# A decoder layer on one core: more of a threshold search and a square on ScalarE, down weights prepared earlier and kept in DRAM

## The chip, the cores and the metric

One core of a Trainium2 chip. The metric is the device time of one execution in microseconds (us), the median of several runs. PE is TensorE, PEld its weight load, DVE is VectorE, ACT is ScalarE, POOL is GpSimd, SP is SyncE, which issues the DMAs. L12 is line 12 of the kernel.

## The reference, cut to what matters

One layer over 2048 tokens of width 1024 in float32. A query keeps 256 keys, chosen by an indexer's scores; attention runs over those keys; its output is normalised per head. Then comes a SwiGLU with 2816 hidden columns.

```python
score = jnp.where(causal[None], score, NEG_INF)
_, sel = lax.top_k(score, k_sel)                # k_sel = 256
...                                             # attention over the selected keys
attn = group_rms_norm(attn, attn_norm_g, N_HEADS_ATTN)   # x * rsqrt(mean(x*x) + eps) per head
x = layer_norm(DEEPNORM_ALPHA * x + g1[:, None, :] * mix, ln1_g[l], ln1_b[l])
ff = (silu(h @ w_gate) * (h @ w_up)) @ w_down   # h = modulate(x, sh2, sc2)
x = layer_norm(DEEPNORM_ALPHA * x + g2[:, None, :] * ff, ln2_g[l], ln2_b[l])
```

## The kernel before, in words

Tokens are 16 blocks of 128 (P = 128, CH = 512). The program is written as nested generators. A planner, which works with its own costs, turns it into one fixed order of instructions for each engine; every engine then runs its list in order and waits at semaphores. So an instruction that waits holds up all that stands behind it on that engine. The same holds for SP, on whose list nearly all DMAs stand (`dma` is `nc.sync.dma_start`). A tile that takes over memory from another one waits for that tile's last reader.

**Search (`topk`, L458 to 569).** The 256th largest score of every query is found by a threshold search: in each of 8 iterations the columns of a block above the threshold are counted. A block b has n = 128(b + 1) columns. ScalarE counts the last n2 of them with Sign and an accumulator (L512), VectorE the first n1 = n - n2 with a comparison and an accumulator (L514). n2 is one number for a group of blocks; DVE_SHARE = 0.42 sets it. The groups (2 to 5), (6 to 8), (9, 10) are searched early. LATE, (11, 12, 13) and (14, 15), are searched as background work of the attention loop: scores come back from DRAM as tile scb, and `attention` calls `next(background)` once a step.

**Attention (L821 to 1049).** It has 136 steps of one query block and 128 keys: three matmuls for each half of the heads into l, exp on ScalarE into p (L894), its half-precision copy ph (L895), the rest pr on POOL (L897), 24 small matmuls into o (L907 to 909). `maxima` (L863 and 865: TensorE, then a reduction on VectorE) runs ahead for the next blocks. `finish` (L911 to 924) copies o to ov, squares it into asq (L916, VectorE), sums, and scales.

**Feed-forward.** Products are Strassen-like: a 2 x 2 block product in 7 products, HM = (1, 2, 6, 5, 7, 3, 4), whose operands are sums of blocks; each operand is split in a high and a low half-precision part (`split_w`: ACT copy L215, DVE L216), and each product runs as three matmuls. Gate and up: 11 pairs p of hidden tiles, for each two groups of rows, grp 0 and 1, which I call units; a unit is 7 x 2 x 12 = 168 matmuls (L1207). `hidden1` makes products 1, 2, 6, 5, `hidden2` 7, 3, 4. In grp 1 the weights of the next pair are prepared (`prep_w`). `put_g` writes the combined activations to DRAM (go, L1237 to 1242). PSUM has 8 banks, all used in turn.

Down: 8 passes q of 7 products, each 11 pairs times 3 matmuls, so 231 (L1503). The left operands, gi, come back from DRAM into 4 buffers. Pass 0 goes by pieces of pairs (0 to 3, 4 to 7, 8 to 10), all 7 products in each. The 77 right operands stay in SBUF for all passes: 24 tiles wdr where the activations of group 0 lay, 8 wdw in the weight buffers, 2 wdt, 43 wdo in the pool fo, which opens when the pools of gate and up close. `prep_wd` makes them (L1388 to 1407): per pair 4 raw loads, 4 sums on POOL (L1105 to 1112), 7 splits. 24 tiles are asked for after the last unit of group 0, the rest inside pass 0, as needed. Raw buffers, sums, temporaries and output buffers are rings with a few slots each; from the start of gate and up the raw ring has 8 and the output ring 6.

Of the kernel before, what the change touches and what calls it, by code (L numbers as in the profile page):

```python
# [12 lines left out]
F16 = mybir.dt.float16  # L13
# [8 lines left out]
P = 128  # L22
# [120 lines left out]
def body(ctx: ExitStack, tc: tile.TileContext, A, out, force=False):  # L143
# [13 lines left out]
    xn_d = [dram(f"xn_d{b}", [P, D], F32) for b in range(NB)]  # L157
    h2_d = [dram(f"h2_d{b}", [P, KT * P], F32) for b in range(NB)]
    t_d = {m: dram(f"t_d{m}", [P, 2, 4, CH], F16) for m in HM[3:]}
    g_d2 = [{m: dram(f"gg_d{g}_{m}", [P, 4, NP, 2, P], F16) for m in HM} for g in range(2)]  # L160


# [295 lines left out]
    def topk(blocks, scs):  # L458
# [34 lines left out]
        V.scalar_tensor_tensor(hi[:, 0], sd, 8.0, mu, op0=ALU.mult, op1=ALU.add)  # L493
        zero, below = sm("zero")[:, 0], sm("below")[:, 0]

        n2 = int(sum(b + 1 for b in blocks) / nb * P * (1 - DVE_SHARE)) // 64 * 64
        big_at, tgt = TOPK - n2 / 2.0, TGT - n2 / 2.0
        V.tensor_scalar(lo[:, 1], cst(C_N), -n2 / 2.0, None, op0=ALU.add)
        V.memset(hi[:, 1], -n2 / 2.0)
# [6 lines left out]
        for it in range(NITER):  # L506
            for i, b in enumerate(blocks):
                n = (b + 1) * P
                n1 = n - n2
                j1 = tk.tile([P, 1024], BF16, tag="j1", name="j1", bufs=1)  # L510
                j2 = tk.tile([P, 1216], BF16, tag="j2", name="j2", bufs=1)
                S_.activation(j2[:, 0:n2], scs[i][:, n1:n], AF.Sign, bias=t[:, i:i + 1],  # L512
                              scale=-1.0, accum_out=ca2[:, i:i + 1])
                V.tensor_scalar(j1[:, 0:n1], scs[i][:, 0:n1], t[:, i:i + 1], None,  # L514
                                op0=ALU.is_ge, op1=ALU.add, accum_out=cd[:, i:i + 1])
                yield
            V.scalar_tensor_tensor(cnt, ca2, -0.5, cd, op0=ALU.mult, op1=ALU.add)
            V.scalar_tensor_tensor(which, tcur[:, 1:2].broadcast_to([P, 2, nb]), big_at, upper,
                                   op0=ALU.is_ge, op1=ALU.not_equal)
            V.copy_predicated(ends, which.bitcast(I32).unsqueeze(2).broadcast_to([P, 2, 2, nb]),  # L520
                              tcur.unsqueeze(1).broadcast_to([P, 2, 2, nb]))
            if it == NITER - 1:
                break
            V.tensor_tensor(dd, hi, lo, op=ALU.subtract)
            d = dd[:, 0]
            if it == 0:
                V.scalar_tensor_tensor(a, cnt, -tgt, sd, op0=ALU.add, op1=ALU.mult)
                V.tensor_tensor(a, a, cst(C_SL), op=ALU.mult)
                V.tensor_tensor(a, a, t, op=ALU.add)
                V.scalar_tensor_tensor(f, d, 0.02, lo[:, 0], op0=ALU.mult, op1=ALU.add)  # L530
                V.tensor_tensor(a, a, f, op=ALU.max)
                V.scalar_tensor_tensor(f, d, -0.02, hi[:, 0], op0=ALU.mult, op1=ALU.add)
                V.tensor_tensor(t, a, f, op=ALU.min)
            else:
                V.reciprocal(a, dd[:, 1])
                V.scalar_tensor_tensor(f, lo[:, 1], -tgt, a, op0=ALU.add, op1=ALU.mult)
                V.tensor_scalar(f, f, CLIP - 1.0, -CLIP, op0=ALU.max, op1=ALU.min)
                V.tensor_tensor(f, f, d, op=ALU.mult)
                V.tensor_tensor(t, lo[:, 0], f, op=ALU.subtract)
            if it == PROBE:  # L540
                V.tensor_scalar(a, lo[:, 0], 0.0, None, op0=ALU.is_lt)
                V.scalar_tensor_tensor(f, hi[:, 0], 0.0, a, op0=ALU.is_gt, op1=ALU.mult)
                V.copy_predicated(t, f.bitcast(I32), zero)
            if it == PROBE + 1:
                V.tensor_scalar(f, hi[:, 0], 0.0, None, op0=ALU.is_equal)
                V.copy_predicated(t, f.bitcast(I32), below)
            yield
# [273 lines left out]
    def attention(pool=None, background=None, at_block=None, at_end=None):  # L821
# [89 lines left out]
        def finish(b, po):  # L911
            ov = aq[0].tile([P, 2, 4, 65], F32, tag="ov", name=f"ov{b}", bufs=two)
            S_.activation(ov, po[:, :, 0:260].rearrange("p g (h d) -> p g h d", d=65), AF.Copy)
            o3 = ov.rearrange("p g h d -> p (g h) d")
            sq = aq[0].tile([P, H, DH], F32, tag="asq", name=f"asq{b}", bufs=1)
            V.tensor_tensor(sq, o3[:, :, 0:64], o3[:, :, 0:64], op=ALU.mult)  # L916
            ms = ap.tile([P, 2, H], F32, tag="ms", name=f"ms{b}", bufs=2)
            V.tensor_reduce(ms[:, 0], sq, axis=AX.X, op=ALU.add)
            V.tensor_tensor(ms[:, 1], o3[:, :, 64], o3[:, :, 64], op=ALU.mult)
            V.scalar_tensor_tensor(ms[:, 0], ms[:, 1], EPS * DH, ms[:, 0], op0=ALU.mult, op1=ALU.add)  # L920
            root(ap, ms[:, 0], ms[:, 0], 1.0 / DH, None)
            on = ap.tile([P, H, DH], F32, tag="on", name=f"on{b}", bufs=three)
            V.tensor_tensor(on, o3[:, :, 0:64], ms[:, 0].unsqueeze(2).broadcast_to([P, H, DH]), op=ALU.mult)
            return on
# [451 lines left out]
    def wd_slots(R):  # L1376
        for n in range(24):
            yield R.tile([P, 2, CH], F16, name=f"wdr{n}")
        for n in range(8):
            yield wring(f"wdw{n}")  # L1380
        for n in range(2):
            yield outs(f"wdt{n}").rearrange("p a x t -> p (a x t)").rearrange("p (x n) -> p x n", x=2)
        n = 0
        while True:
            yield fo[0].tile([P, 2, CH], F16, name=f"wdo{n}")
            n += 1

    def prep_wd():  # L1388

        R = ff.enter_context(tc.tile_pool(name="fw", bufs=1, side="right", reuse_waits="tile"))  # L1390
        gpool[0] = R
        slots = wd_slots(R)
        for p in range(NP):
            b = []
            for r in range(2):
                for hh in range(2):
                    x = raws(f"wd{p}_{r}{hh}")
                    dma(x, A["wd"][2 * p + r][:, hh * CH:(hh + 1) * CH])
                    b.append(x)
            y = sums(f"yd{p}")  # L1400
            for m in RIGHT:
                x = right(G, b, y, m)
                w = next(slots)
                split_w(w[:, 0], w[:, 1], x)
                wd_tiles[m, p] = w
                yield p

    rows = {}
    fo = [None]
    gpool = [None]  # L1410
    pwd = prep_wd()
    second = prep_h(1)
    for p in range(NP):
        nxt = {}
        pw = prep_w(p + 1, nxt) if p + 1 < NP else iter(())
        for grp in range(2):
            if p == 0 and grp == 0:
                u, v, g11 = heads["u"], heads["v"], heads["g"]
                gate = temps("gate")
                gated(gate, g11, 0)  # L1420
                gated(g11, heads["c"][1], 1, gate)
            else:
                u, v = [temps(f"u{grp}{p}_{x}") for x in range(2)], {}
                g11 = prods(f"g11_{grp}{p}")
                for i, _ in enumerate(hidden1(fbank, Ws, HT[grp], u, v, g11, lambda k, x: temps(f"{k}h{grp}{p}_{x}"))):
                    if grp == 1 and i % 2:
                        if i == 1:
                            next(pw, None)
                        next(pw, None)
            for i, _ in enumerate(hidden2(fbank, Ws, HT[grp], u, v, g11, p, grp)):  # L1430
                if grp == 1 and i % 2 and p:
                    next(pw, None)
                if p == 0 and grp == 0 and i == 0:
                    for _ in second:
                        pass
            if p == NP - 1 and grp == 0:
                early_h[0].close()
                for _ in range(24):
                    next(pwd)
        if p == 0:  # L1440
            few_s.close()
            fq = hid.enter_context(tc.tile_pool(name="fq", reuse_waits="tile", bufs=1))
            wring.slots[8:12] = [(fq, 4)] * 4
        for _ in pw:
            pass
        Ws = nxt
# [44 lines left out]
        G.tensor_tensor(x, x, rows["l1b"][hh], op=ALU.add)  # L1491
        return x

    PIECES = ((0, 4), (4, 8), (8, 11))

    def down(q, m, ps, p0, p1_):
        g = gpool[0].tile([P, 4, 2, P], F16, tag="gi", name=f"gi{q}_{m}{p0}", bufs=4)[:, 0:p1_ - p0]
        dma(g, g_d2[q // 4][m][:, q % 4, p0:p1_])
        for p in range(p0, p1_):
            while (HM[-1], p) not in wd_tiles or (HM[-2], p) not in wd_tiles:  # L1500
                next(pwd)
            for n, (x, y) in enumerate(((0, 0), (0, 1), (1, 0))):
                T.matmul(ps, g[:, p - p0, x], wd_tiles[m, p][:, y], start=p == 0 and n == 0,  # L1503
                         stop=p == NP - 1 and n == 2)
# [1 line left out]
    for q in range(8):  # L1506
        blocks = (q // 4 * 8 + q % 4, q // 4 * 8 + q % 4 + 4)
        banks = {}
        if q == 0:
            banks = {m: fbank() for m in HM}  # L1510
            for piece in PIECES:
                for m in HM:
                    down(q, m, banks[m], *piece)
# [121 lines left out]
```

## Time and profile before

| | us |
|---|---|
| median of 3 runs (2542.55 to 2549.05) | 2543.98 |
| the profiled execution | 2544.64 |
| its span | 2542.8 |
| PE busy | 2319.4 (91%) |
| DVE busy | 1804.2 (71%) |
| ACT busy | 1185.0 (47%) |
| POOL busy | 1230.5 (48%) |

The span is what the profiler recorded from the first to the last instruction. Busy times overlap; an engine that is busy or idle matters only where the next step waits for it. Times inside the kernel are us from the span's start.

### The profile page before, as it was taken

What the parts mean: (1) busy time and instruction counts of PE and PEld (TensorE: products, weight loads), DVE (VectorE), ACT (ScalarE), POOL (GpSimd) and SP (SyncE); (2) the same over time, 40 slices, a digit from 0 to 9 for tenths busy, and PEclk for the clock granted to TensorE, in tenths of its full rate; (3) what the DMA queues carried; (4) which work ended last, traced back from release to release, by engine and by line L of the source; (5) the groups of instructions that cost most, each with busy time, mean ns of one, the idle gap of its engine ahead of it and who ended that gap; (6) DMA issues with size and microseconds to landing.
All of it is one profiled execution on the core that took longest, in us unless ns stands there. A gap on an engine that the chain in (4) does not pass through costs nothing.

```text
span 2542.8 us, 38397 instructions
## 1 busy us (share of the span) xinstructions
PE 2319.4 (91%) x13538; PEld 1119.3 (44%) x13538; DVE 1804.2 (71%) x3649; ACT 1185.0 (47%) x2263; POOL 1230.5 (48%) x1232
## 2 busy tenths in 40 slices
PE   5799999996879699889969999999999986999998
PEld 3444444443444355555424444444444432444443
DVE  8998999989999876763396666776666697422223
ACT  3687776646767566777543233332333343110000
POOL 3000000003655666898376556655655565855455
PEclk9799999998989899999979999999999998999999
DMA  8421442434131322330242223222222236444443
GB/s 272 127 104 68 149 133 89 150 123 144 58 121 60 126 93 81 117 110 29 106 132 88 75 87 92 84 71 75 71 88 79 85 115 207 150 141 148 128 137 121
DMA packets 213917, 281.72 MB, mean 111 GB/s; under 512 B 15825, under 2 KB 128849, under 8 KB 212945
## 3 DMA queue, kind: packets, MB, share of 16 engines
q1 hardware_dynamic: 213712, 279.17, 34.5%
q8 instruction: 107, 1.75, 0.3%
q14 instruction: 98, 0.79, 0.1%
HBM read 183.20 MB, written 95.91 MB: 110 GB/s over the span
## 4 chain that ended last, share of the span: by engine, by line
PE 35%; POOL 6%; DMA 4%; DVE 3%; issue 2%; ACT 0%; SPq 0%; DVEq 0%; POOLq 0%
PE f L1207 30%; PE f L1503 5%; DMA x<-xn_d 2%; POOL z L1480 1%; DMA gi<-gg_d 1%; POOL x L1491 1%; POOL x L1490 1%; POOL z L1547 1%; POOL z L1548 1%; DMA wd<-in_wd 1%; DVE wdo L216 0%; DVE h L1171 0%; DVE z L1536 0%; POOL wd L1112 0%; POOL yd L1105 0%
## 5 line engine op out<-in xcount | busy, mean ns | idle before, releaser
L897 POOL TENSOR_TENSOR pr<-p,ph 128x256 f16<-128x256 f32 x544 | 379.6, 730 | 140.2 <-ACT ph L895 61.2
L1207 PE MATMUL f<-h,wwg 128*128 128x512 f16 x1800 | 419.9, 383 | 25.0 <-ACT h L1170 18.0
L1207 PE MATMUL f<-h,wwu 128*128 128x512 f16 x1800 | 414.1, 380 | 0.0
L1241 POOL TENSOR_TENSOR go<-g,go 128x512 f16<-128x512 f32 x126 | 169.7, 1356 | 274.1 <-ACT go L1240 236.3
L1503 PEld LDWEIGHTS <-gi 128*128 128x128 f16 x1848 | 180.7, 99 | 276.2 <-DMA gi<-gg_d 47.4
L1207 PEld LDWEIGHTS <-wwg 128*128 128x128 f16 x1848 | 182.1, 99 | 232.3 <-issue 14.9
L1207 PEld LDWEIGHTS <-wwu 128*128 128x128 f16 x1848 | 181.1, 98 | 234.2 <-issue 17.0
L1503 PE MATMUL f<-wdo,gi 128*128 128x512 f16 x1032 | 242.1, 386 | 15.6 <-DMA gi<-gg_d 6.8
L865 DVE CUSTOM_DVE_ANT_0 jk<-m,ua 128x512 bf16<-128x512 f32 (+3 forms) x320 | 193.7, 605 | 56.2 <-PE m L863 41.6
L894 ACT ACTIVATE p<-l 128x512 f32<-128x512 f32 x272 | 158.3, 598 | 90.7 <-PE l L890 69.2
L1240 ACT ACTIVATE go<-g 128x512 f16<-128x512 f32 x132 | 82.5, 627 | 230.6 <-issue 82.8
L447 ACT ACTIVATE r<-xs 128x512 f32<-128x512 f32 (+3 forms) x304 | 153.4, 548 | 57.3 <-PE xs L446 14.0
L895 ACT ACTIVATE ph<-p 128x512 f16<-128x512 f32 x272 | 166.5, 635 | 2.9
L909 PE MATMUL o<-vst,pr 128*128 128x65 f16 x1088 | 140.4, 196 | 14.4 <-POOL pr L897 13.7
L1503 PE MATMUL f<-wdr,gi 128*128 128x512 f16 x576 | 136.5, 386 | 16.2 <-DMA gi<-gg_d 16.1
L737 PE MATMUL b<-hi,wch 128*128 128x512 f16 x384 | 146.7, 382 | 0.0
L737 PE MATMUL b<-lo,wch 128*128 128x512 f16 x384 | 146.3, 381 | 0.0
L737 PE MATMUL b<-hi,wcl 128*128 128x512 f16 x384 | 146.3, 381 | 0.0
L907 PE MATMUL o<-vst,ph 128*128 128x65 f16 x1088 | 142.8, 194 | 1.8 <-ACT ph L895 1.8
L908 PE MATMUL o<-vst,ph 128*128 128x64 f16 x1088 | 141.5, 194 | 0.0
L1470 ACT ACTIVATE frs<-fmv,epsw 128x1 f32<-128x1 f32 x16 | 4.7, 294 | 282.3 <-DVE fmv L1467 282.3
L863 PE MATMUL m<-k1T,qst 128*128 128x512 f16 (+3 forms) x320 | 105.4, 360 | 29.5 <-DVE mp L865 26.0
(384 smaller groups left out, 5194.3 us busy)
## 6 DMA issues: line engine op xcount, KB each, us to landing
gg_d<-go SPq DMA_DIRECT2D x154, 256.0 KB, 2.6
gi<-gg_d SPq DMA_DIRECT2D x112, 256.0 KB, 3.0
wa<-in_w_ada SPq DMA_DIRECT2D x64, 256.0 KB, 2.9
wg<-in_wg SPq DMA_DIRECT2D x49, 256.0 KB, 3.0
wu<-in_wu SPq DMA_DIRECT2D x49, 256.0 KB, 3.0
wd<-in_wd SPq DMA_DIRECT2D x44, 256.0 KB, 3.0
gi<-gg_d SPq DMA_DIRECT2D x56, 192.0 KB, 2.8
wa<-in_w_ada SPq DMA_DIRECT2D x16, 512.0 KB, 8.6
```

The lines of the kernel that those rows point to most:

```text
L447: S_.activation(r[:, i:i + e], ps[:, 0:e], AF.Relu)
L737: T.matmul(ps, w[:, k, j * P:(j + 1) * P], x[:, k], start=n == 0, stop=n == 3 * KT - 1)
L865: V.tensor_tensor_reduce(jk[:, 0:w], ps[:, 0:w], u[:, j * 512:j * 512 + w], scale=1.0, scalar=-3e38, op0=ALU.add, op1=ALU.max, accum_out=m ...
L894: S_.activation(p32, pl_, AF.Exp, scale=DH ** -0.5)
L895: S_.activation(ph, p32, AF.Copy)
L897: G.tensor_tensor(pr[:, i:i + CH // 2], p32[:, i:i + CH // 2], ph[:, i:i + CH // 2], op=ALU.subtract)
L907: T.matmul(o, lhs, vst[:, kt, 64:129], start=kt == 0 and hh == 0, stop=False)
L908: T.matmul(o[:, 0:64], lhs, vst[:, kt, 0:64], start=False, stop=False)
L909: T.matmul(o, pr[:, hh * P:(hh + 1) * P], vst[:, kt, 64:129], start=False, stop=kt == b and hh == 3)
L1207: T.matmul(ps, w[:, x, k * P:(k + 1) * P], h[:, y, :, k], start=n == 0, stop=n == 11)
L1241: (V if (p, grp) in LASTG else G).tensor_tensor(o[:, :, 1], x4, o[:, :, 0], op=ALU.subtract)
L1503: T.matmul(ps, g[:, p - p0, x], wd_tiles[m, p][:, y], start=p == 0 and n == 0, stop=p == NP - 1 and n == 2)
```

## The change

Four edits. (a) In the searches of LATE, n2 becomes b0 * P, with b0 the first block of the group: 1408 columns for blocks 11 to 13 and 1792 for 14 and 15. (b) The square in `finish` moves from VectorE to ScalarE. (c) `prep_wd(p)` becomes a generator for one pair; it is stepped beside the products of group 0 of pair p + 1 (for the last pair beside group 1), at every second of their yields, and stores each tile to a DRAM tile wd_d. (d) `load_wd` loads the tiles in the order in which pass 0 uses them: 24 after the last unit of group 0, the others ahead of pass 0, the first 28 of these in fo. In pass 0 the gi loads are issued by ScalarE. The scratch tiles of the counts change their size (j1, j2).

```diff
+    wd_d = {(m, p): dram(f"wd_d{m}_{p}", [P, 2, CH], F16) for m in HM for p in range(NP)}
...
-        n2 = int(sum(b + 1 for b in blocks) / nb * P * (1 - DVE_SHARE)) // 64 * 64
+        if blocks in LATE:
+            n2 = b0 * P
+        else:
+            n2 = int(sum(b + 1 for b in blocks) / nb * P * (1 - DVE_SHARE)) // 64 * 64
...
-                j1 = tk.tile([P, 1024], BF16, tag="j1", name="j1", bufs=1)
-                j2 = tk.tile([P, 1216], BF16, tag="j2", name="j2", bufs=1)
+                j1 = tk.tile([P, 640], BF16, tag="j1", name="j1", bufs=1)
+                j2 = tk.tile([P, 1792], BF16, tag="j2", name="j2", bufs=1)
...
-            V.tensor_tensor(sq, o3[:, :, 0:64], o3[:, :, 0:64], op=ALU.mult)
+            S_.activation(sq, o3[:, :, 0:64], AF.Square)
...
     def wd_slots(R):
         for n in range(24):
             yield R.tile([P, 2, CH], F16, name=f"wdr{n}")
+        for n in range(28):
+            yield fo[0].tile([P, 2, CH], F16, name=f"wdo{n}")
         for n in range(8):
             yield wring(f"wdw{n}")
-        for n in range(2):
-            yield outs(f"wdt{n}").rearrange(...)
-        n = 0
+        n = 28
...
-    def prep_wd():
+    def prep_wd(p):
...
+        yield                                   # after the 4 raw loads
+        y = sums(f"yd{p}")
+        for m in RIGHT:
+            x = right(G, b, y, m)
+            w = outs(f"wdp{p}_{m}").rearrange(...)
+            split_w(w[:, 0], w[:, 1], x)
+            dma(wd_d[m, p], w)
+            yield
+
+    def load_wd():
+        gpool[0] = ff.enter_context(tc.tile_pool(name="fw", bufs=1, side="right", reuse_waits="tile"))
+        slots = wd_slots(gpool[0])
+        for piece in PIECES:
+            for m in HM:
+                for p in range(*piece):
+                    wd_tiles[m, p] = next(slots)
+                    dma(wd_tiles[m, p], wd_d[m, p])
+                    yield
...
+            pd = iter(())
+            if grp == 0 and p:
+                pd = prep_wd(p - 1)
+            elif grp and p == NP - 1:
+                pd = prep_wd(p)
...                                             # in the loops over hidden1 and hidden2:
+                    if i % 2 == 0:
+                        next(pd, None)
...
+            for _ in pd:
+                pass
...
-        dma(g, g_d2[q // 4][m][:, q % 4, p0:p1_])
+        (S_.dma_start if q == 0 else dma)(g, g_d2[q // 4][m][:, q % 4, p0:p1_])
...
-            while (HM[-1], p) not in wd_tiles or (HM[-2], p) not in wd_tiles:
-                next(pwd)
...
             banks = {m: fbank() for m in HM}
+            for _ in pwd:
+                pass
```

## Rows read from the trace of the kernel before

**Rows 1.** Busy time by stage; the first line names the columns.
```profile
core 0: us, PE busy (x) PEld busy (x) DVE busy (x) ACT busy (x) POOL busy (x), PEclk, DMA share, GB/s
...
604.00:860.00 256.00, 204.13 (x1779) 111.87 (x1778) 238.62 (x686) 179.03 (x354) 146.39 (x193) 0.91 0.27 91
860.00:1268.00 408.00, 376.93 (x3662) 214.04 (x3660) 251.45 (x605) 272.67 (x557) 299.09 (x407) 0.99 0.27 93
...
1321.00:1930.30 609.30, 608.77 (x2807) 275.33 (x2807) 416.13 (x499) 198.04 (x340) 353.17 (x253) 0.99 0.28 84
1930.30:1966.50 36.20, 36.20 (x169) 16.46 (x168) 18.76 (x24) 8.98 (x16) 16.05 (x13) 1.00 0.22 66
1966.50:2002.80 36.30, 36.30 (x170) 16.43 (x168) 29.89 (x35) 14.93 (x26) 25.79 (x19) 1.00 0.32 95
...
2039.00:2075.30 36.30, 36.30 (x170) 16.46 (x168) 35.96 (x32) 17.73 (x32) 31.23 (x20) 1.00 0.39 116
2075.30:2168.10 92.80, 62.54 (x227) 23.40 (x225) 70.18 (x84) 35.65 (x62) 48.01 (x32) 0.83 0.52 168
2168.10:2532.60 364.50, 353.41 (x1624) 157.21 (x1622) 104.49 (x171) 33.62 (x55) 198.45 (x154) 1.00 0.47 139
```

**Rows 2.** Waits of PE, 604 to 860: waiter, releaser, us, times, longest.
```profile
PE m L863 <- DVE mp L865: 11.4, 15, 1.9
PE m L875 <- DVE mx L871: 9.6, 4, 6.0
...
PE m L965 <- DVE z L957: 7.6, 4, 4.6
```

**Rows 3.** Groups of DVE by line and shape, 604 to 860: busy us, mean ns, idle before.
```profile
L514 DVE TENSOR_SCALAR_CACHE_REDUCE j<-scb,tc 128x832 bf16<-128x832 f32 x16 | 17.2, 1074 | 0.2
...
L514 DVE TENSOR_SCALAR_CACHE_REDUCE j<-scb,tc 128x960 bf16<-128x960 f32 x8 | 9.7, 1208 | 0.1
L514 DVE TENSOR_SCALAR_CACHE_REDUCE j<-scb,tc 128x704 bf16<-128x704 f32 x8 | 7.4, 930 | 0.0
...
L514 DVE TENSOR_SCALAR_CACHE_REDUCE j<-scb,tc 128x576 bf16<-128x576 f32 x8 | 6.4, 802 | 0.0
L916 DVE TENSOR_TENSOR asq<-ov 128x512 f32<-128x512 f32 x8 | 6.1, 765 | 0.0
```

**Rows 4.** The same view of DVE, 0 to 604.
```profile
L514 DVE TENSOR_SCALAR_CACHE_REDUCE j<-sc,tc 128x192 bf16<-128x192 f32 x8 | 3.3, 410 | 0.2
```

**Rows 5.** The same view of ACT: 604 to 860, and L754 from 0 to 604.
```profile
L512 ACT ACTIVATE j<-scb,tc 128x960 bf16<-128x960 f32 x24 | 26.1, 1090 | 7.2 <-DVE tc L539 4.0 <-DVE tc L546 2.8 <-DVE tc L491 0.3
L512 ACT ACTIVATE j<-scb,tc 128x1088 bf16<-128x1088 f32 x16 | 19.2, 1198 | 7.2 <-DVE tc L543 2.9 <-DVE tc L539 2.5 <-DVE tc L533 1.0
...
L754 ACT ACTIVATE g<-y 128x512 f32<-128x512 f32 x16 | 10.1, 628 | 14.4 <-DVE y L753 14.3
```

**Rows 6.** Groups by line in the last unit, 2039 to 2075.3: DVE, POOL, ACT.
```profile
L216 DVE SCALAR_TENSOR_TENSOR wdr<-wd,wdr 128x512 f16<-128x512 f32 x18 | 24.7, 1398 | 0.1
...
L1110 POOL TENSOR_TENSOR wd<-yd,wd 128x512 f32<-128x512 f32 x4 | 6.8, 1715 | 0.6 <-DVE wdr L216 0.6
...
L215 ACT ACTIVATE wdr<-wd 128x512 f16<-128x512 f32 x20 | 11.7, 622 | 11.6 <-DMA wd<-in_wd 4.8 <-POOL wd L1108 3.9 <-POOL wd L1110 1.9
```

**Rows 7.** SP's queue in order of time: start, duration, DMA issued.
```profile
2076.50 9.23 SPq L1398 DMA_DIRECT2D wd<-in_wd  x4
...
2092.21 0.33 SPq L1498 DMA_DIRECT2D gi<-gg_d  x1
...
2105.92 0.44 SPq L1460 DMA_DIRECT2D l1g<-in_ln_g  x1
```

**Rows 8.** Waits of PE in pass 0, then in passes 1 to 7.
```profile
PE f L1503 <- DMA gi<-gg_d: 21.0, 9, 8.9
...
PE f L1503 <- DMA gi<-gg_d: 10.9, 16, 1.5
```

**Rows 9.** Busy time by stage, columns as in rows 1: a stretch at the kernel's start.
```profile
10.00:40.00 30.00, 18.65 (x88) 10.47 (x89) 29.46 (x62) 9.67 (x17) 8.37 (x8) 0.94 1.07 362
```

More of the change, by code (lines that the diff above doesn't have):

```diff
@@ L1378, in wd_slots @@
             yield R.tile([P, 2, CH], F16, name=f"wdr{n}")
+        for n in range(28):
+            yield fo[0].tile([P, 2, CH], F16, name=f"wdo{n}")
         for n in range(8):
             yield wring(f"wdw{n}")
-        for n in range(2):
-            yield outs(f"wdt{n}").rearrange("p a x t -> p (a x t)").rearrange("p (x n) -> p x n", x=2)
-        n = 0
+        n = 28
         while True:
@@ L1386, in wd_slots @@
             n += 1
-    def prep_wd():
[L1390 to L1406, printed above, removed]
+    def prep_wd(p):
+        b = []
+        for r in range(2):
+            for hh in range(2):
+                x = raws(f"wd{p}_{r}{hh}")
+                dma(x, A["wd"][2 * p + r][:, hh * CH:(hh + 1) * CH])
+                b.append(x)
+        yield
+        y = sums(f"yd{p}")
+        for m in RIGHT:
+            x = right(G, b, y, m)
+            w = outs(f"wdp{p}_{m}").rearrange("p a x t -> p (a x t)").rearrange("p (x n) -> p x n", x=2)
+            split_w(w[:, 0], w[:, 1], x)
[10 more added lines that the diff above has]
+                    yield
     rows = {}
@@ L1410, in body @@
     gpool = [None]
-    pwd = prep_wd()
+    PIECES = ((0, 4), (4, 8), (8, 11))
+    pwd = load_wd()
     second = prep_h(1)
@@ L1432, in body @@
                     next(pw, None)
+                if i % 2 == 0:
+                    next(pd, None)
                 if p == 0 and grp == 0 and i == 0:
@@ L1492, in residual @@
         return x
-    PIECES = ((0, 4), (4, 8), (8, 11))
     def down(q, m, ps, p0, p1_):
         g = gpool[0].tile([P, 4, 2, P], F16, tag="gi", name=f"gi{q}_{m}{p0}", bufs=4)[:, 0:p1_ - p0]
-        dma(g, g_d2[q // 4][m][:, q % 4, p0:p1_])
+        (S_.dma_start if q == 0 else dma)(g, g_d2[q // 4][m][:, q % 4, p0:p1_])
         for p in range(p0, p1_):
-            while (HM[-1], p) not in wd_tiles or (HM[-2], p) not in wd_tiles:
-                next(pwd)
             for n, (x, y) in enumerate(((0, 0), (0, 1), (1, 0))):
```

## Prediction

> **What bounds the kernel now.** I read the stage table first: busy time of each engine, stage by stage, because the share of one engine over the whole span mixes stages with different limits [rows 1]. Four of its rows matter here. In the stage 604 to 860 us, where attention starts while the top-k search of blocks 11 to 15 runs behind it, VectorE is busy 238.62 of 256 us (93%) and ScalarE 179.03: VectorE is the limit. In 860 to 1268 it is TensorE (376.93 of 408). In gate and up TensorE has no gap at all: 608.77 of 609.30, and 36.20 of 36.20 and 36.30 of 36.30 in the units after it. A unit (pair p, row group) is 168 matmuls, so one matmul takes 36.3/168 = 0.216 us. In the down product the first pass (q=0) takes 92.80 us for 231 matmuls, which at 0.216 would be 50; the other seven take 364.50 for 1617, which would be 349. So there are three places where time can be had: the VectorE stage, 43 us of the first pass, 15 us of the other passes.
>
> Second view, the waits. In 604 to 860 the longest waits of TensorE for another engine are for VectorE [rows 2]. In the first pass TensorE waits 21.0 us for activations (gi), not for weights, and in passes 1 to 7 10.9 us [rows 8]. The reader should not stop at the name gi: the queue of SP shows why gi is late. SP is in order, and four raw weight loads occupy it from 2076.50 for 9.23 us, waiting for raw buffers that the preparation of earlier weights still holds; the fifth gi load is only issued at 2092.21, behind them [rows 7]. The first pass is bounded by the preparation of the down weights.
>
> **Part A, the search and the square.** The ScalarE share of the columns rises from 960 to 1408 in blocks 11 to 13, and from 1088 to 1792 in 14 and 15; VectorE keeps 128, 256, 384, 128 and 256 columns. Eight iterations each. VectorE counts these now in 17.2 + 9.7 + 7.4 + 6.4 = 40.7 us [rows 3]; the line through 576 columns (0.802) and 960 (1.208) has 1.057 ns a column, so 128, 256 and 384 columns cost 0.33, 0.46 and 0.60; the row for 192 columns (0.410, the line gives 0.40) bears this out [rows 4]. That makes 8 x 1.39 + 8 x 0.79 = 17.4, so VectorE loses 23.3 us. ScalarE: (1.198 - 1.090)/128 = 0.84 ns a column [rows 5], so 1408 columns take 1.47 and 1792 take 1.79; 24 x 1.47 + 16 x 1.79 = 63.9 in place of 26.1 + 19.2 = 45.3: ScalarE gains 18.6. The square leaves VectorE 8 times in this stage (6.1 us, [rows 3]) and comes to ScalarE at 0.628 each [rows 5], 5.0 us. It follows its input ov on the same engine, so it waits for nobody; behind it stand exponentials, and the reduction on VectorE now waits for it. The other eight squares lie where TensorE is the limit and count nothing.
>
> So VectorE goes to 238.6 - 23.3 - 6.1 = 209, ScalarE to 179.0 + 23.6 = 203, of 256. The gain lies between 0 (the room is filled by ScalarE, whose exponentials now stand behind counts of up to 1.8 us) and the whole 29 us that VectorE loses. Other row: TensorE's three longest waits for VectorE here sum to 28.6 us [rows 2], and 12% of VectorE's work is taken away, which by itself would give back only 3 to 4. I take **12**, about the middle.
>
> The Trainium skill (ScalarE: Activation LUTs, Rules for kernel authors) says that plain arithmetic belongs on VectorE, which it calls up to about three times faster per element in bf16; by that rule this part would gain nothing. The rows differ for these f32 counts: 0.84 ns a column on ScalarE against 1.06 on VectorE.
>
> **Part B, the down weights.** Per pair p the preparation is 4 raw loads, 4 POOL sums, 7 ScalarE copies, 7 VectorE splits; the change adds 7 stores and 7 loads of 256 KB. It moves from the last unit and the first pass into the units of group 0 (p = 1 to 10), and for pair 10 into the last unit.
>
> Cover in gate and up: at the prices of the last unit, where all three engines are crowded (splits 1.398, copies 0.622, sums 1.715 [rows 6]), a unit gets 9.8 us of VectorE, 4.4 of ScalarE, 6.9 of POOL. A group-0 unit has 18.76, 8.98 and 16.05 of 36.20 [rows 1], so it goes to 28.6, 13.3 and 22.9. The neighbouring group-1 unit already runs 29.89, 14.93 and 25.79 with TensorE at 36.30 of 36.30, and the last unit carries 22 splits (three times as many) and VectorE at 35.96, TensorE still without a gap. I cost it at **0**; bounds 0 and 11 (1 us for each of 11 units, should a store hold one of the six output buffers too long). SP gets 18 more issues a pair at 0.3 to 0.5 us, under 9 us in 72.
>
> First pass: no lower than 50 us. 77 weight tiles (20.2 MB) now come by DMA, and 21 gi loads (5.0 MB). 24 tiles and 4 gi have space as soon as the activations of group 0 are dropped, at about 2039; 7.3 MB in the last unit's 36 us is 203 GB/s, with the 116 that run there [rows 1] 319, so they are in place at about 2075. Remaining: 53 tiles and 17 gi, 17.9 MB. The rate: 362 GB/s at the kernel's start [rows 9]; the first pass now moves 168 GB/s at a share of 0.52 [rows 1], so 323 at full share; 17.9 MB take 49 to 55 us. When may they start? The next 28 tiles lie where the seven activation tiles of group 1 lay. If each is given back as TensorE finishes it, 24 come during the last unit, the rest (11.6 MB, 36 us) hides, and the pass takes 50 + 3 for start and landing: 53. If the pool opens only when its last user is done: the first load into it now is issued at 2105.92 [rows 7], 31 us after the last gate matmul, when VectorE has cleared splits and tail. Without the splits the tail is some 24 VectorE operations of 0.68, 16 us: loads from 2091 to 2140 or 2146, last tiles used by 2149, so 69 to 74. I take **62**, the middle: 92.8 - 62 = 31 us gained. The gi loads of this pass go to ScalarE's queue, out of SP's way; they wait for one of four buffers, that is for 12 matmuls, 2.6 us; behind them on ScalarE stand the last copies, whose consumers (VectorE, then stores for q = 4 and up) have time.
>
> Passes 1 to 7: the gi wait of 10.9 comes from SP's order in these passes, which stays; POOL no longer does sums and residuals at once. Between 349 and 365; I take 363, a gain of **1.5**.
>
> **Sum**, against the profiled execution: its span is 2542.8, its time 2544.64. 2542.8 - 12 - 31 - 1.5 = 2498.3, with 1.8 outside the span 2500.1. The median of the three runs lies 0.7 below the profiled one; I say **2500**.
>
> **The rivals.** (1) Forecast, 2485 to 2512: chance 0.45. (2) The first pass becomes bound by loads. For: with SP unblocked, 53 loads are issued in some 17 us at 0.33 each [rows 7], while 53 transfers take 43; 30 stand waiting, 25 us, and a gi load that queues behind them lets four buffers run dry. Against: gi comes from another queue; no row shows a ScalarE queue. Then four gi per round trip of 15 to 25 us, and a pass of 80 to 93: 2518 to 2531, say 2522; chance 0.17. The Trainium skill (DMA: Bandwidth & Descriptors, Queues, rings and completion order) has each DMA engine take turns between the rows of SP and ScalarE, which would keep gi out of that backlog; no run here shows it yet. (3) Part A pays nothing: ScalarE takes over as the limit of that stage (203 us plus waits), the rest as forecast: 2512; chance 0.15. (4) Both at their good ends, 27 and 40: 2476; chance 0.12. (5) Slower: the cover in gate and up fails. A store of a weight tile waits in SP's queue, an output buffer stays taken, ScalarE's copy stands before the tanh, VectorE does not drain PSUM, TensorE stops. Each unit would have to lose 44.5/11 = 4.0 us before the whole is slower; at 5 us it is 2555. Against it stands the last unit, full and without a gap [rows 1]; chance 0.05. (6) It does nothing: gains and new waits cancel, 2537 to 2551; chance 0.06.
>
> **How the numbers follow.** Predicted 2500, the forecast's. The range 2479 to 2527 leaves out (5), (6), about half of (4) and a fifth of (2), together some 0.2. A measurement of this kernel tells 0.3%, 7.6 us, from no change: faster than 2536.4 are (1) to (4), 0.89, of which I keep 0.88 for what I have not seen; same 0.06, slower 0.06.
>
> **What would show it.** Part A: the stage from 604 to the end of the second late search shorter by about 12 us, counts of 1.47 and 1.79 on ScalarE, VectorE under 90%. Part B: group-0 units of 36.2 us with TensorE full and VectorE near 28; the first pass at 62; no wait of TensorE for VectorE or ScalarE weights in it, its waits, if any, for DMA. The prediction is wrong if a gap appears in gate and up, if ScalarE is full in 604 to 860, or if the first pass stays above 80.

## The result, and the profile after

The changed kernel takes 2508.74 us (median; 2506.58 to 2509.76), the kernel before 2545.03 on the same chip: ratio 0.9859 [0.9844, 0.9873], 36 us faster (32 to 40). The forecast was 2500, with 2479 to 2527 as the range. The profiled execution after has a span of 2504.4 us, 38.4 less than before.

First view, the stage table of the changed kernel, cut at its own boundaries; columns as in [rows 1].

```profile
core 0: us, PE busy (x) PEld busy (x) DVE busy (x) ACT busy (x) POOL busy (x), PEclk, DMA share, GB/s
604.00:860.00 256.00, 216.69 (x1884) 118.08 (x1883) 215.42 (x677) 204.12 (x376) 148.69 (x201) 0.92 0.26 85
...
1312.00:1920.40 608.40, 607.13 (x2807) 274.94 (x2807) 474.30 (x552) 224.98 (x395) 407.79 (x286) 1.00 0.39 122
1920.40:1956.70 36.30, 36.30 (x170) 16.48 (x169) 25.52 (x33) 12.89 (x22) 20.93 (x16) 1.00 0.39 123
...
2029.30:2065.60 36.30, 36.30 (x170) 16.43 (x168) 24.58 (x35) 12.50 (x23) 14.98 (x11) 1.00 0.98 342
2065.60:2133.70 68.10, 56.06 (x232) 22.66 (x231) 14.96 (x22) 4.54 (x7) 12.36 (x10) 0.95 0.91 315
2133.70:2493.70 360.00, 351.76 (x1618) 156.88 (x1616) 94.42 (x161) 31.38 (x52) 186.65 (x146) 1.00 0.46 138
```

Beside [rows 1]: in 604 to 860 VectorE falls from 238.62 to 215.42 and ScalarE rises from 179.03 to 204.12. TensorE has no gap in a group-0 unit (36.30 of 36.30), although VectorE has 25.52 in place of 18.76 there. The last unit's VectorE falls from 35.96 to 24.58. Pass 0 goes from 92.80 to 68.10, and in it VectorE, ScalarE and POOL have little left to do (14.96, 4.54 and 12.36 us) while the DMA share goes from 0.52 to 0.91.

Where the 38.4 us lie, from the ends of the stages:

| place | before | after | gain, us | forecast |
|---|---|---|---|---|
| start of the down product (A, and gate and up) | 2075.35 | 2065.63 | 9.7 | 12 and 0 |
| pass 0 | 92.75 | 68.1 | 24.6 | 31 |
| passes 1 to 7 | 364.5 | 360.0 | 4.5 | 1.5 |
| behind them | 10.2 | 10.7 | -0.5 | 0 |

Second view, groups of VectorE and ScalarE by line and shape, 604 to 860, columns as in [rows 3, 5].

```profile
L518 DVE TENSOR_SCALAR_CACHE_REDUCE j<-scb,tc 128x256 bf16<-128x256 f32 x16 | 7.6, 476 | 0.3
...
L518 DVE TENSOR_SCALAR_CACHE_REDUCE j<-scb,tc 128x128 bf16<-128x128 f32 x16 | 5.5, 343 | 0.3
...
L518 DVE TENSOR_SCALAR_CACHE_REDUCE j<-scb,tc 128x384 bf16<-128x384 f32 x8 | 4.9, 607 | 0.1
```
```profile
L516 ACT ACTIVATE j<-scb,tc 128x1408 bf16<-128x1408 f32 x24 | 35.4, 1474 | 7.5 <-DVE tc L547 3.6 <-DVE tc L543 1.7 <-DVE tc L550 1.1
L516 ACT ACTIVATE j<-scb,tc 128x1792 bf16<-128x1792 f32 x16 | 28.6, 1790 | 12.4 <-DVE tc L492 5.6 <-DVE tc L550 3.7 <-DVE tc L537 1.7
...
L920 ACT ACTIVATE asq<-ov 128x512 f32<-128x512 f32 x8 | 5.1, 634 | 0.1
```

The counts cost what the straight lines through [rows 3, 5] gave: VectorE 18.0 us (forecast 17.4), ScalarE 64.0 (63.9), the square 5.1 (5.0).

Third view, around pass 0: what TensorE waits for (waiter, releaser, us, times, longest), in pass 0 of the kernel before beside the gi wait of [rows 8], then in 2065.6 to 2133.7 of the changed one; then SP's queue in order of time. In this last view one row runs from the first to the last issue of a series, waits between them included.

```profile
PE f L1503 <- DVE wdo L216: 5.0, 8, 1.0
PE f L1503 <- ACT wdo L215: 3.7, 4, 1.2
```
```profile
PE f L1522 <- DMA gi<-gg_d: 9.6, 5, 2.6
PE f L1522 <- DMA wdo<-wd_d: 2.2, 6, 0.5
```
```profile
2071.48 2.69 SPq L1246 DMA_DIRECT2D gg_d<-go  x2
2074.26 0.58 SPq L1406 DMA_DIRECT2D wd_d<-wdp  x1
2074.89 36.70 SPq L1416 DMA_DIRECT2D wdo<-wd_d  x45
```

TensorE waits for no weight from VectorE or ScalarE any more; all its waits are for DMA. The wait of 9.23 us for raw buffers in [rows 7] is gone. In its place 45 weight loads start 9.3 us after the last matmul of gate and up (2065.63), and SP is at them for 36.7 us, 0.82 us a load, against 0.33 for a lone issue in [rows 7]. The issues themselves are no slower. The first line below has the durations of the 45 (ns: least, median, most), the second what SP waits for between them:

```profile
L1416 SPq DMA_DIRECT2D wdo<-wd_d x45: 319/320/1004, 2074.9 to 2111.3; - x45
SPq L1416 <- DMA wdo<-wd_d: 14.3, 25, 1.5
```

The median issue takes 0.32 us. Between issues SP waits, by the trace for earlier loads to land. The next view, the stage table by tens of us, shows that the DMA engines have no room for more.

```profile
2075.00:2085.00 10.00, 9.28 (x42) 3.85 (x41) 0.00 (x0) 0.00 (x0) 0.00 (x0) 1.00 0.97 334
...
2105.00:2115.00 10.00, 6.34 (x21) 2.16 (x21) 0.00 (x0) 0.00 (x0) 0.00 (x0) 0.83 1.05 386
2115.00:2125.00 10.00, 4.97 (x22) 1.99 (x23) 3.59 (x5) 1.88 (x2) 5.56 (x5) 1.00 0.95 342
2125.00:2135.00 10.00, 10.00 (x40) 4.14 (x39) 4.66 (x7) 0.00 (x0) 6.83 (x6) 0.83 0.34 101
```

The DMA engines are full from 2075 to 2125, and TensorE runs short towards the end, until they have caught up. Of the 68.1 us TensorE waits for 11.8 and is busy for 56.06, though its 231 matmuls take 50 at the 0.216 us of the forecast: 2125 to 2135 is filled by 40 of them, at a granted clock of 0.83. **The theory after the result:** part A gives some 10 us through the counts; pass 0 is now bounded by DMA bytes that don't start to flow before the memory of gate and up is free. The experiments take the parts of this one by one.

### The profile page after: what moved, and what is told of

It is laid out like the page before. It is cut to its first block, busy times and chain, and to the rows that moved or that the text cites. A ratio compares the mean times of both kernels' runs of the same rounds, so it can differ in the third digit from the quotient of the medians.

```text
span 2504.4 us, 38645 instructions
## 1 busy us (share of the span) xinstructions
PE 2320.2 (93%) x13538; PEld 1123.5 (45%) x13538; DVE 1773.0 (71%) x3633; ACT 1201.5 (48%) x2279; POOL 1228.0 (49%) x1232
## 5 line engine op out<-in xcount | busy, mean ns | idle before, releaser
L1245 POOL TENSOR_TENSOR go<-g,go 128x512 f16<-128x512 f32 x126 | 164.3, 1311 | 224.8 <-ACT go L1244 114.0
L1522 PE MATMUL f<-wdo,gi 128*128 128x512 f16 x1080 | 247.7, 381 | 9.8 <-DMA gi<-gg_d 7.4
L913 PE MATMUL o<-vst,pr 128*128 128x65 f16 x1088 | 141.8, 197 | 14.3 <-POOL pr L901 13.5
L1522 PE MATMUL f<-wdr,gi 128*128 128x512 f16 x576 | 131.4, 379 | 4.6 <-DMA gi<-gg_d 4.6
```

The lines of the kernel that those rows point to most:

```text
L913: T.matmul(o, pr[:, hh * P:(hh + 1) * P], vst[:, kt, 64:129], start=False, stop=kt == b and hh == 3)
L1245: (V if (p, grp) in LASTG else G).tensor_tensor(o[:, :, 1], x4, o[:, :, 0], op=ALU.subtract)
```

## Part A: counts and square, apart and together

Four kernels. `counts_only` and `square_only` are the kernel before with one of the two edits, `a_both` has both and nothing of the down weights, `no_square` is the changed kernel without the square.

```diff
 # counts_only, a_both: kernel before
-        n2 = int(sum(b + 1 for b in blocks) / nb * P * (1 - DVE_SHARE)) // 64 * 64
+        if blocks in LATE:
+            n2 = b0 * P
...
 # square_only, a_both: kernel before; no_square: the changed kernel, the other way
-            V.tensor_tensor(sq, o3[:, :, 0:64], o3[:, :, 0:64], op=ALU.mult)
+            S_.activation(sq, o3[:, :, 0:64], AF.Square)
```

> The kernel before with the counts of blocks 11 to 15 moved (1408 and 1792 columns on ScalarE), nothing else. In the changed kernel gate and up start 8.8 us earlier than before. Theory: VectorE was the limit of the stage from 604 to 860 us, and the counts are 23 of the 29 us taken from it there; so most of the 8.8 comes from them: 6 to 9 us faster than before, VectorE busy about 221 in that stage. Rival: ScalarE fills up with the counts (198 busy) and holds the exponentials back, the gain is the square's: 0 to 2 us faster or slower than before.

> The kernel before with the square of the attention output on ScalarE, nothing else. Theory: 6 us of VectorE in the stage where it is the limit, out of 29: 1 to 2 us faster. Rival: the square sits in the chain at the end of each of 16 blocks (copy, square, sum, root), and one hop between engines falls away 16 times: 6 to 9 us faster.

> The kernel before with the counts and the square moved, and nothing of the down weights. The counts alone gave -6.4 us (ratio 0.9975), the square alone nothing (1.0002). Theory that the two simply add: -6 to -7 us, 0.9973 to 0.9978. Theory that the square pays only once the counts are gone from VectorE (together they take 29 us of it, apart 23 and 6): -9 to -12 us, 0.9953 to 0.9965. If the square on ScalarE stands in the way of the counts there, the two give less than the counts alone: above 0.998.

> The changed kernel with the square back on VectorE; the counts stay on ScalarE, the down weights stay as changed. Theory that the square pays nothing: the ratio of the changed kernel, 0.984 to 0.9875. Theory that the square pays beside the counts: 3 to 5 us more than the changed kernel, a ratio of 0.987 to 0.989. The first pass of the down product stays at 67 to 69 us in either.

| kernel | us | ratio to before |
|---|---|---|
| counts_only | 2541.96 | 0.9975 [0.9965, 0.9985] |
| square_only | 2550.01 | 1.0002 [0.9992, 1.0013] |
| a_both | 2537.9 | 0.9960 [0.9947, 0.9973] |
| no_square | 2512.72 | 0.9865 [0.9850, 0.9881] |

The counts give 6.4 us by themselves, the square alone nothing. Together they give 10.2 us (7 to 13), close to what the changed kernel shows at the start of the down product (9.7). The square beside the counts is then worth 4 us by the middle values in the first comparison and 1.5 in the second (0.9865 against 0.9859), with intervals that overlap in both. Whether it is worth anything in time stays open; the counts carry this part.

The profiles of all twelve runs, the later ones included, point the same way. In 604 to 860 TensorE does 203.4 to 204.2 us of work without the counts moved, with or without the square (before, `square_only`, `b_only`), 212.3 and 212.7 with the counts alone, and 214.8 to 217.2 in the seven with both. So once the counts are gone the square does let TensorE do more in this stage. But the down product starts at 2075.4 to 2078.9, at 2069.3 and 2071.6, and at 2065.6 to 2071.7 in these three sets: there the second and the third can't be told apart, and the 9.7 of the one pair is good to a few us.

Why 10, where VectorE was relieved of 23.2 us in this stage? The stage itself gained more than 10. By 860 TensorE has done 216.69 us of work in place of 204.13, 12.6 more. What follows takes some of it back, about 6 us in 884 to 924 (below). The stage table again, two stretches of the kernel before and then of the changed one:

```profile
844.00:884.00 40.00, 26.77 (x159) 12.79 (x158) 30.15 (x63) 21.35 (x44) 24.28 (x23) 0.76 0.42 139
884.00:914.00 30.00, 29.40 (x275) 16.74 (x274) 19.88 (x52) 20.08 (x44) 22.80 (x32) 1.00 0.35 116
```
```profile
844.00:884.00 40.00, 35.17 (x325) 20.18 (x322) 34.56 (x61) 29.62 (x56) 34.49 (x43) 0.87 0.40 128
884.00:914.00 30.00, 23.08 (x193) 13.20 (x191) 27.57 (x60) 22.12 (x48) 26.17 (x27) 0.77 0.39 137
```

Before, TensorE starves in 844 to 884 (26.77 of 40). After, it doesn't there, but in the 30 us behind, where VectorE is busy 27.57 and the granted clock falls to 0.77. What fills VectorE and ScalarE there is the preparation for gate and up (wwg, wwu, h); the longest wait of ScalarE in either kernel is for a sum of it from POOL, and exponentials stand behind that wait:

```profile
ACT wwg L215 <- POOL ywg L1094: 5.4, 1, 5.4
```
```profile
ACT wwg L216 <- POOL ywg L1098: 6.6, 1, 6.6
```

(the first in 840 to 890 of the kernel before, the second in 880 to 915 after). So the thin stretch moved behind the search rather than vanished. In 884 to 924 TensorE is busy 38.92, 38.93 and 37.38 of 40 us in the profiles of the kernel before, of `square_only` and of `b_only` (below), and between 32.3 and 33.1 in those of all nine runs with the counts moved. It isn't the square, then. No run took this preparation away, so that it is what costs the rest is read from the profile, not shown.

## Part B alone

The changed kernel with the counts and the square as before.

```diff
-        if blocks in LATE:
-            n2 = b0 * P
-        else:
-            n2 = int(...)
+        n2 = int(...)
...
-            S_.activation(sq, o3[:, :, 0:64], AF.Square)
+            V.tensor_tensor(sq, o3[:, :, 0:64], o3[:, :, 0:64], op=ALU.mult)
```

> The changed kernel with counts and square put back as before: the down weights alone. Theory: the parts lie in stages that TensorE's full gate and up separate, so they add: 29 us faster than before (24.6 in pass 0, 4.5 in passes 1 to 7), pass 0 at 68. Rival: part of the gain needs the other part (more room on VectorE during the preparation): below 24 us, with VectorE waits in the group-0 units.

2528.23 us, ratio 0.9922 [0.9899, 0.9946]: 20 us (14 to 26). The theory had said 29, and the interval leaves that out. The rival had said below 24 with TensorE waiting for VectorE in the group-0 units. Gate and up lost nothing: from its first matmul to the first of the down product the profile takes 845.2 us, as that of the kernel before does, and the one wait of TensorE for VectorE in it, 3.3 us for h, is in both. The down product, from its first matmul to its last, takes 431.1 us against 456.7 before, 25.6 less; pass 0 takes 66.8, so what is missing of the 29 lies in passes 1 to 7 (364.7 us). Together with `a_both` the run gives 30 (21 to 39) against the 36 (32 to 40) of the whole: the parts add, within what the intervals tell.

## The gi loads back on SP

```diff
-        (S_.dma_start if q == 0 else dma)(g, g_d2[q // 4][m][:, q % 4, p0:p1_])
+        dma(g, g_d2[q // 4][m][:, q % 4, p0:p1_])
```

> The changed kernel with the 21 gi loads of pass 0 back on SP's queue. Pass 0 took 68.1 us in the changed kernel, the DMA engines 91% busy. Theory: the bytes bind (18 MB at 340 GB/s), but on SP every gi load waits for a buffer that TensorE gives back and holds up the weight loads behind it, so the DMA engines run dry between: pass 0 at 75 to 90, the whole 7 to 20 us slower than the changed kernel. Rival: all DMAs share the same engines, the issuing queue does not matter: pass 0 at 66 to 70, the whole within 3 us of the changed kernel.

2524.47 us, ratio 0.9906 [0.9885, 0.9927]: 12 us slower than the changed kernel. Pass 0 takes 80.2. The longest wait of TensorE in pass 0, and SP's queue:

```profile
PE f L1522 <- DMA gi<-gg_d: 27.6, 1, 27.6
```
```profile
2078.98 0.38 SPq L1519 DMA_DIRECT2D gi<-gg_d  x1
2079.42 29.70 SPq L1416 DMA_DIRECT2D wdo<-wd_d  x45
2109.53 2.35 SPq L1519 DMA_DIRECT2D gi<-gg_d  x4
```

This is rival (2), and it is real: one wait of 27.6 us for a load that SP had not even issued, because 45 weight loads stood ahead of it on its list. The expectation had the time right and the order the wrong way round: it had gi loads hold up weight loads. ScalarE's queue avoids the wait. Of the whole gain of 36 us, 12 hang on where 21 of the loads are issued.

## Fewer bytes

The 21 down weights of pairs 8 to 10 are not loaded; the products of these pairs use the tiles of pairs 4 to 6.

```diff
+                    if p >= 8:
+                        wd_tiles[m, p] = wd_tiles[m, p - 4]
+                        continue
                     wd_tiles[m, p] = next(slots)
                     dma(wd_tiles[m, p], wd_d[m, p])
```

> The changed kernel without the last 21 weight loads: the products of pairs 8 to 10 use the weights of pairs 4 to 6, so 5.5 MB of DMA are left out and TensorE's work stays the same. Theory: pass 0 is bound by the bytes that the DMA engines still have to bring after the pool opens (45 weight tiles and 17 gi, 340 GB/s), so it shrinks by nearly 5.5/0.34 = 16 us, to 52 to 55, near TensorE's 50. Rival: gi is what TensorE waits for (17.8 of 20.0 us of its waits in the down product), and its four buffers and ScalarE's queue set the pace; then pass 0 stays at 64 to 68.

2504.02 us, ratio 0.9817 [0.9801, 0.9833]; pass 0 takes 60.6. That lies between the two expectations. SP's queue and the waits of TensorE in pass 0:

```profile
2078.02 22.99 SPq L1419 DMA_DIRECT2D wdo<-wd_d  x28
```
```profile
PE f L1525 <- DMA gi<-gg_d: 3.9, 2, 2.2
PE f L1525 <- DMA wdo<-wd_d: 3.0, 6, 1.3
```

Leaving out 5.5 MB (21 tiles of 262 kB), worth 15 us at the 368 GB/s that the changed kernel moves in 2075 to 2115, shortened the pass by 7.5. So bytes do bound it, but the run doesn't show that they alone do: the 28 tiles of the first two pieces still start 9.7 us after the last unit (2068.28) and still make TensorE wait. The start of the loads had to be moved.

## Loads that start earlier

`early_release` gives the tiles no pool of their own. Down weights are loaded into quarters of the activation tiles that gate and up have finished with (one tile holds four), and they are asked for inside the loops of the last two units. The gi buffers lie in the last activation tile of group 0. The 8 tiles wdw and 17 tiles of fo stay as they were.

```diff
+    fh = ctx.enter_context(tc.tile_pool(name="fh", reuse_waits="tile", bufs=1))
+    held_h(fh, 1, HM)
...
-        for n in range(24):
-            yield R.tile([P, 2, CH], F16, name=f"wdr{n}")
-        for n in range(28):
-            yield fo[0].tile([P, 2, CH], F16, name=f"wdo{n}")
+        for g, ms in ((0, HM[:6]), (1, HM)):
+            for m in ms:
+                for n in range(4):
+                    yield quarter(HT[g][m], n).rearrange("p a k t -> p a (k t)")
...
+                elif p == NP - 1 and (grp, i) != (0, 5):
+                    for _ in range(4):
+                        next(pwd)
```

> The changed kernel, but the first 52 weight tiles are loaded into the activation tiles themselves, four into each as soon as its product of the last pair is done, and the gi buffers into the last one of group 0; no pool has to open first. The loads are stepped beside the products of the last two units. Same bytes. Theory: the loads start some 26 us earlier, at about 1999, where the DMA share is only 0.41 to 0.44 (18 us each), so pass 0 gets down to 52 to 57 and the whole is 10 to 16 us faster than the changed kernel. Rival: the DMA engines are full anyway from 2035 on, and loads that start early only delay the stores and the preparation of the last pair: pass 0 at 64 or more, gain under 4 us, or gaps of TensorE in the last two units.

2490.26 us, ratio 0.9769 [0.9753, 0.9785]: 59 us faster than before and, by the two ratios, some 23 faster than the changed kernel. Its stage table, from the last group-0 unit to the end of pass 0:

```profile
1994.40:2012.00 17.60, 17.60 (x83) 7.99 (x82) 12.09 (x12) 7.38 (x13) 14.65 (x11) 1.00 0.58 175
2012.00:2031.00 19.00, 19.00 (x89) 8.59 (x88) 15.60 (x21) 4.56 (x8) 8.60 (x8) 1.00 1.00 328
2031.00:2049.00 18.00, 18.00 (x85) 8.18 (x84) 10.72 (x14) 7.72 (x14) 13.95 (x10) 1.00 1.03 345
2049.00:2067.50 18.50, 18.50 (x87) 8.39 (x86) 14.34 (x24) 4.93 (x9) 1.59 (x1) 1.00 1.06 387
2067.50:2121.30 53.80, 50.54 (x232) 22.17 (x231) 14.41 (x22) 4.48 (x7) 10.33 (x9) 1.00 0.87 303
2121.30:2475.50 354.20, 350.41 (x1618) 157.52 (x1616) 94.23 (x161) 30.82 (x52) 188.76 (x147) 1.00 0.46 141
```

The DMA engines are full from 2012 on, under two units in which TensorE has no gap, and pass 0 is 53.8 us, TensorE busy 50.54 of them. That is the good end of the forecast (53). The whole gains more than the 10 to 16 us expected: pass 0 gives 14.3 of it against the changed kernel, passes 1 to 7 another 5.8, with 3.8 us of gi wait in place of 8.1. Why passes 1 to 7 gain, no run separates; the gi buffers lie elsewhere in this kernel.

This run had changed two things, the memory and the place of the request. `late_ask` keeps the memory and asks where the changed kernel asks; `early_again` is `early_release` once more beside it.

```diff
 # late_ask, against early_release
-                elif p == NP - 1 and (grp, i) != (0, 5):
-                    for _ in range(4):
-                        next(pwd)
...
+            if p == NP - 1 and grp == 0:
+                for _ in range(24):
+                    next(pwd)
```

> The down weights are loaded into the activation tiles themselves, as in early_release, but asked for where the changed kernel asks for them: 24 after the last unit of group 0, the others after the last unit. In early_release the loads are asked for inside the loops of the last two units, so that run had changed two things at once, the memory and the place of the request. If memory that opens as a whole was what held the loads of the changed kernel back until 2074.89, then this run is as good as early_release: loads for group 1's tiles spread over the last unit, first pass 53 to 57 us, ratio 0.976 to 0.979. If the place in the program, and so the order on SP's list behind the last stores of the activations and weights, held them back, the loads start 9 to 12 us after the last unit again and the first pass takes 64 to 70 us, ratio 0.983 to 0.988.

> early_release once more, on the chip of late_ask, so that the two stand beside each other: ratio 0.975 to 0.979, first pass 53 to 55 us.

`late_ask` 2492.16 us, 0.9772 [0.9756, 0.9788]; `early_again` 2491.63, 0.9764 [0.9747, 0.9780]. They are the same. In the profile of `late_ask` pass 0 takes 54.2 us, and its SP queue shows both kinds of memory side by side:

```profile
2005.79 0.60 SPq L1419 DMA_DIRECT2D h<-wd_d  x1
...
2019.58 7.03 SPq L1419 DMA_DIRECT2D h<-wd_d  x12
...
2066.66 2.29 SPq L1419 DMA_DIRECT2D h<-wd_d  x4
...
2079.73 0.59 SPq L1410 DMA_DIRECT2D wd_d<-wdp  x1
2080.66 15.15 SPq L1419 DMA_DIRECT2D wdo<-wd_d  x17
```

Asked for late, the loads into activation tiles (h) still stand early on SP's list, from 2005.79 on, though the last unit of group 0, behind which the program asks for them, ends at 2032.4: the planner has moved them forward. The 17 loads into fo start at 2080.66, 11.8 us after the last unit (2068.9; 9.3 in the changed kernel). So it was the memory, not the place of the request. In either kernel the last store of a prepared weight (wd_d) stands right ahead of the first load into fo, at 2074.26 and 2079.73, and in the changed kernel SP goes from the one to the other without a wait: while the kernel ran, the place on SP's list behind the last stores held the loads back. Whether the planner put them there because the pool opens as a whole or because its tiles lie over buffers that the tail still uses, no run separates.

## Why the prediction was right or wrong, point by point

**Direction and place** were right: VectorE in the search stage, the preparation of down weights in pass 0, and nothing lost in gate and up.

**Part A, forecast 12, got 10.** The prices of the instructions were right to 4%. That 12 was near is in part luck: "about the middle" between 0 and 29 was no working. It met 12.6 us at 860, of which the thin stretch behind the search takes some back. The prediction's [rows 2] could not show this stretch, as its window ended at 860. Of the two edits the counts do the work; that the square's 6.1 us leave VectorE could be read, but not that they give nothing by themselves.

The Trainium skill (ScalarE: Activation LUTs, Rules for kernel authors) names VectorE for simple arithmetic such as add and mul, with a figure for bf16; carried over to these counts, the rule would keep them there. The run with the counts alone differs from it, by 6.4 us of gain, where VectorE is the full engine and a column of f32 more costs a count 0.84 ns on ScalarE against 1.06 on VectorE (the slopes of [rows 3, 5]).

**Gate and up, forecast 0, got 0:** 36.30 of 36.30 with the preparation added. The cover named, a last unit without a gap at 35.96 us of VectorE, was the right row to go by.

**Pass 0, forecast 62, got 68.1: the term that was mis-sized,** by 6 us, the largest miss of the sum (part A was 2 us too high, passes 1 to 7 3 us too low). The prediction gave two ends for the start of the 28 tiles in fo, tile by tile (53) and only when the last user is done (69 to 74), and took the middle. The trace showed the second one: loads at 2074.89, 9.3 us after the last gate matmul, where the prediction had worked out 16; 45 of them, where it had 53, as the eight tiles in the weight buffers were loaded in the last unit; and 368 GB/s where it had taken 323 to 362. So the late end came out slightly better than its bounds. A middle between two mechanisms was the error: 62 is a time that neither gives. The row for l1g in [rows 7], the evidence named for the late one, says little on when the pool opens: ScalarE's first write into a tile of it (wdo) stands at 2103.7 in the same trace, and both are in lists behind other work. The late end was the one that came, and 69 its nearer value; with it, and the other terms as they were, the forecast is 2507. `early_release` and `late_ask` show that the other end exists too: 53.8 and 54.2 against 53. The prediction also read the first pass of the kernel before as waiting "for activations (gi), not for weights": the same view has 8.7 us of waits for tiles wdo from VectorE and ScalarE (third view), beside the 21.0 for gi. Both went with the preparation, so the step held.

**Rival (2)** was named for the right reason and needed one more fact. The prediction had 53 loads issued in 17 us and standing in a queue behind SP. In the trace SP issues one in 0.32 us but waits between issues for earlier loads to land, so the loads stand on SP's list, and a gi load on the same list waits for all of them: 27.6 us in `gi_on_sp`. Its pass of 80.2 is the lower bound of that rival (80 to 93), reached by one long wait and not by four gi per round trip as the rival had it; that the numbers meet is luck. The Trainium skill (DMA: Bandwidth & Descriptors, Queues, rings and completion order) has each DMA engine take turns between the rows of SP and ScalarE. The changed kernel fits this: the 256 KB gi loads that ScalarE issued in pass 0 landed after 5.4 us (median of 10), the wdo loads on SP's queue after 5.3. But as SP waits for its own loads to land, no run here has a deep queue on one row, and the rule itself wasn't put to the proof.

**Passes 1 to 7, forecast 1.5, got 4.5** in this pair of profiles. Both lie between the bounds of 349 and 365. The gi wait fell from 10.9 to 8.1, POOL's work from 198.45 to 186.65. But 4.5 is more than the edit gives. In the kernel before, six of the 231 matmuls of pass 0 come behind 2168.1, where pass 1 starts with 12 of its own; by count the passes differ by 3.2. And from the 232nd matmul of the down product to the end of the last, the four runs without the edits of the down weights take 362.1 to 364.8 us, the five with them and with the gi buffers of the changed kernel 359.9 to 364.7. So the forecast of 1.5 is not contradicted. `early_release` reaches 354.2, with 3.8 us of that wait.

## What to carry to other kernels

When work is replaced by loads, ask first when the memory that they go to is free: here 45 loads that started only 9 us after the last unit made pass 0 14 us longer than it is with loads straight into dead tiles (68.1 against 53.8), more than all of part A gave. Loads that a running product waits for must not share an in-order list with a bulk load; another queue was worth 12 us. Where the rows leave two mechanisms with two prices, forecast one of them and give the other its chance: the middle (62) is a time that neither gives (68.1 and 53.8).

## What the runs showed of the hardware that was not expected

A backlog of loads shows up as time of the issuing list, though an issue nearly keeps its price. It took 0.33 us alone [rows 7], and with the DMA engines full 0.32 in the median of the 45 and 0.43 in that of the 17 of `late_ask`. But a load left SP only every 0.82 us there (45 in 36.70 us), every 0.66 in `gi_on_sp` (29.70) and every 0.89 in `late_ask` (17 in 15.15 us), because in these programs SP waits between issues, by the traces mostly for earlier loads to land: 14.3 us in 25 waits, and 13.0 in 36 in `gi_on_sp`. At 5.3 us from issue to landing and 0.82 from load to load, some six were under way at a time (an estimate). At a DMA share of 0.97 to 1.06 the core's DMA engines moved 328 to 387 GB/s.

In the changed kernel TensorE's granted clock was 0.77 in 884 to 914, a mean of stretches at its level of 2.4 GHz (1.00 in 875 to 890) and at that of 1.2 GHz (0.50 in 895 to 905, after it had been busy only 2.17 of the 5 us before); in the same 30 us of the kernel before it was 1.00, with TensorE busy 29.40. In the stretch in which TensorE starves, its work also takes longer: a matmul of k2T and q into `l` (L894) took 634 ns in 895 to 905, the same one (L890) 381 in 884 to 914 of the kernel before.
